# A two-layer encoder trunk: residual stream kept feature-major, with the RMS factor of each token taken as a column sum on TensorE

## The chip, the cores and the metric

One core of a Trainium2 chip. The metric is the device time of one execution of the whole program in microseconds. The engines have their own instruction queues and run side by side: TensorE (PE, with its weight loads listed apart as PEld), VectorE (DVE), ScalarE (ACT), GpSimd (POOL), and SyncE (SP), which here only issues DMAs. Each queue is worked through in order; waits between queues are semaphores.

## The reference

512 tokens of 1024 features, two layers, float32. Every layer is

```
xn = rmsnorm(x, norm_g[i])
y = mixer(xn)                 # layer 0: neighbourhood attention, layer 1: latent attention (MLA)
h = x + y
gate = sigmoid(rmsnorm(h, ple_norm[i]) @ ple_w_gate[i])
x = h + gate * (p[i] @ ple_w_proj[i])
```

and the output is `rmsnorm(x, final_norm)`, where rmsnorm divides each token by the root of its mean square over the 1024 features and multiplies by a gain per feature. Either mixer projects xn to its operands and to z (1024 wide), runs 16 heads, multiplies the 1024 outputs by silu(z) and projects back: `(o * silu(z)) @ w_out`. Layer 0 takes q, k, v from one projection and attends within a window of 8 x 16 on a grid of 8 x 64 tokens. MLA takes a rank-384 and a rank-256 code and a rotary key from xn, norms the codes, and projects them to 16 heads of q (64 + 32 rotary), k and v.

## The kernel before, in words

Every float32 product is made of three matmuls in the rounded format F32R: each operand is split into hi (an ACT copy that rounds) and lo (the rest, a subtraction), and hi·hi, hi·lo and lo·hi are added in PSUM. `load_w` (L67) loads a weight tile of 512 KB on SP's queue, copies hi on ACT (whi, L76) and subtracts lo on POOL (wlo, L77); the buffers are three deep. A product of 128 output rows, 512 columns and 1024 in the sum is 24 matmuls (`proj_T`, L133).

PSUM has eight banks: two for projections ("mm"), two for scores ("S"), three for transposes ("T") and one for head outputs ("O").

Two layouts are in use. Activations that are to be multiplied stand feature-major, [128 features, 512 tokens] times 8 (`xT`, `oT`, each as hi and lo). The residual stream, `res`, stands token-major, four tiles [128 tokens, 1024 features], since a token's square sum is then one ACT instruction with an accumulator (`inv_rms`, L100: ACT square, DVE scale, POOL power), and its factor a scalar per partition. So `rows_to_cols` (L125) and `turn_h` (L612) turn token tiles by TensorE transposes, four to a PSUM bank, with a hi copy on ACT and a lo subtraction on DVE for each bank: 32 transposes for xn of layer 0, 64 for h of both layers (`hg`), 32 for x between the layers (`x1n`).

The program runs thus. **Start** (L579): the operands of PLE(0), x and the gain row g0 are loaded; xn is made and turned; PLE (p @ w_proj) is written to DRAM through `pe`; five z tiles of layer 0 follow (`z_phase`, L144). **Neighbourhood attention** (`na_heads`, L182): per pair of heads, project v, q and k, then two heads; the last three z tiles come behind the last projections. Each pair ends in `combine` (ACT and DVE, L157) and `gated` (L166: POOL multiply by z, ACT hi, POOL lo), which makes one of eight `oT` tiles. **out_proj**: token tiles t by halves n of the output; in the first half four tiles are open, over both "mm" and both "S" banks, and the terms run by weight chunk (`by_chunk`), with order bound by `issue_after` to the last projection. Each result is added to `res` (L361) and turned. **gate_phase**: 8 products per layer, the sigmoid on ACT with the token's factor as its scale (L401), times pe (L402), added to `res` (L404). In layer 0 `done` (L630) then norms and turns x; in layer 1 (L640) it sums squares half by half, scales and writes the output, the last tile in two pieces of 256. **MLA**: `mla_c` makes the codes, norms and turns them (cn) and moves the rotary key rows into two sets of operand buffers by DMAs on SP (`move`, L89); `mla_heads` (L535 on) makes seven z tiles, then group(0) and project(0) (rope on ACT, DVE, POOL; moves of the rotated rows into qe and qo), the eighth z tile, and the heads with the next projections between them.

The tile framework puts instructions into each engine's queue by its own simulated timeline, within the data dependences; `reuse_waits` lets buffers be taken over across pools with waits on the tiles alone.

## Time and profile before

| | us |
|---|---|
| median of three runs | 691.66 (690.6 to 692.21) |
| profiled execution | 690.26 |
| its span | 688.5, granted TensorE clock 0.998 |

The span is from the first to the last recorded event; the other 1.8 us lie outside the recorded events. The profile divides it thus, by windows of the trace (idle is the window less PE's busy time):

| window, us | what runs | PE busy | PE idle |
|---|---|---|---|
| 0 to 21 | loads, PLE(0), xn and its transposes | 11.76 | 9.24 |
| 21 to 54 | rest of PLE(0), five z tiles | 32.97 | 0.03 |
| 54 to 253 | neighbourhood attention | 198.92 | 0.08 |
| 253 to 358 | out_proj and gates of layer 0, codes begin | 104.67 | 0.33 |
| 358 to 433 | codes, z tiles, first projections of MLA | 72.45 | 2.55 |
| 433 to 585 | MLA heads | 147.97 | 4.03 |
| 585 to 677 | out_proj and gates of layer 1 | 91.67 | 0.33 |
| 677 to 689 | last tile, final norm, output | 4.03 | 7.97 |

In a row of the groups, the line, engine and operation are followed by output and inputs with shapes and the count; then the busy time, the mean length of one in ns, and the engine's idle time just before, with what ended it. A row of the chain is a start, a length and what ran. A row of a timeline is the same with the idle time before it in brackets. In the windows each engine has its busy time and count; after the five engines stand the granted clock, the DMA engines' share, and GB/s.

### The profile page before, as it was taken

The numbers are of one execution on the slowest core, as the hardware profiler recorded it, in microseconds if no ns is written. First come the engines' busy times: TensorE is split into PE (matmuls) and PEld (weight loads), VectorE is DVE, ScalarE is ACT, GpSimd is POOL, SyncE is SP. The second block draws the span as 40 slices with busy tenths as digits, with TensorE's granted clock in tenths as the row PEclk, the third lists the DMA queues.
The fourth block names the chain that finished last, engine by engine and source line by source line (L and its number), as shares of the span: only waits on it lengthen the run. The fifth ranks groups of instructions, "written<-read, shape, count | busy, mean of one in ns | idle before, by whom it ended". The sixth has DMA issues, their size and how long they took to land.

```text
span 688.5 us, 10118 instructions
## 1 busy us (share of the span) xinstructions
PE 664.4 (97%) x3580; PEld 566.9 (82%) x3580; DVE 356.3 (52%) x813; ACT 402.1 (58%) x799; POOL 396.7 (58%) x309
## 2 busy tenths in 40 slices
PE   5999999999999999999999998999999999999995
PEld 4789898998988888788899886787888777887885
DVE  4300364647737624633524503788988886055333
ACT  6722576666767562643443634878888878426433
POOL 1753557467575565853044634777789867658511
PEclk9999999999999999999999999999999999999999
DMA  8731423323223127544243344203121201584122
GB/s 324 234 121 62 133 86 104 105 72 97 85 92 108 40 97 301 167 130 135 89 104 107 107 121 116 81 23 93 24 70 37 86 1 68 191 308 154 61 77 92
DMA packets 28642, 77.53 MB, mean 113 GB/s; under 512 B 3632, under 2 KB 6704, under 8 KB 28592
## 3 DMA queue, kind: packets, MB, share of 16 engines
q1 hardware_dynamic: 28592, 76.89, 33.9%
q8 instruction: 28, 0.46, 0.3%
q14 instruction: 22, 0.18, 0.1%
HBM read 65.34 MB, written 8.39 MB: 107 GB/s over the span
## 4 chain that ended last, share of the span: by engine, by line
PE 86%; ACT 5%; DVE 4%; issue 2%; DMA 1%; POOL 1%; SPq 0%; POOLq 0%; DVEq 0%; ACTq 0%
PE ps_mm L96 63%; PE ps_S L96 9%; PE ps_T L122 5%; PE ps_O L96 4%; PE ps_O L335 2%; PE ps_T L323 1%; ACT ex L561 1%; ACT whi L76 1%; DMA x<-x 1%; PE ps_S L288 1%; PE ps_S L287 1%; DVE mx L559 1%; POOL wlo L77 0%; DVE mx L301 0%; ACT pt_hi L83 0%
## 5 line engine op out<-in xcount | busy, mean ns | idle before, releaser
L77 POOL TENSOR_TENSOR wlo<-wraw,whi 128x1024 fp32r<-128x1024 f32 (+3 forms) x96 | 218.3, 2287 | 118.5 <-ACT whi L76 68.4
L76 ACT ACTIVATE whi<-wraw 128x1024 fp32r<-128x1024 f32 (+4 forms) x100 | 97.9, 988 | 97.0 <-PE ps_mm L96 32.1
L563 POOL TENSOR_TENSOR ex<-ex,rc 128x512 f32<-128x512 f32 x64 | 66.2, 1048 | 20.7 <-DVE rc L562 13.9
L96 PE MATMUL ps_mm<-whi,hnT 128*128 128x512 f32 (+1 forms) x272 | 69.7, 377 | 0.0
L96 PEld LDWEIGHTS ps_mm<-whi,hnT 128*128 128x128 f32 x272 | 49.5, 188 | 9.5
L310 POOL TENSOR_TENSOR ex<-ex,rc 128x128 f32<-128x128 f32 (+1 forms) x64 | 34.3, 560 | 38.1 <-DVE rc L306 36.5
L559 DVE TENSOR_REDUCE mx<-ps_S 128x1 f32<-128x512 f32 x64 | 43.7, 685 | 15.3 <-PE ps_S L96 14.3
L96 PE MATMUL ps_mm<-xh,whi 128*128 128x512 f32 x192 | 50.9, 398 | 0.1
L96 PE MATMUL ps_mm<-xh,wlo 128*128 128x512 f32 x192 | 49.1, 391 | 0.0
L561 ACT ACTIVATE ex<-ps_S,mx 128x512 f32<-128x512 f32 x64 | 44.1, 689 | 8.2 <-DVE mx L559 6.7
L96 PE MATMUL ps_mm<-xl,whi 128*128 128x512 f32 x192 | 48.6, 392 | 0.0
L85 DVE TENSOR_TENSOR pt_lo<-ps_T,pt_hi 128x512 fp32r<-128x512 f32 x64 | 43.0, 679 | 5.0 <-ACT pt_hi L83 4.6
L305 ACT ACTIVATE ex<-ex,mx 128x128 f32<-128x128 f32 (+1 forms) x64 | 30.2, 473 | 22.0 <-DVE mx L301 21.6
L106 POOL TENSOR_TENSOR rs<-ss,half 128x1 f32<-128x1 f32 x24 | 13.0, 549 | 50.3 <-DVE ss L105 49.0
L96 PEld LDWEIGHTS ps_mm<-xl,whi 128*128 128x128 f32 x192 | 35.6, 188 | 7.3
L96 PEld LDWEIGHTS ps_mm<-xh,wlo 128*128 128x128 f32 x192 | 35.6, 188 | 7.0
L83 ACT ACTIVATE pt_hi<-ps_T 128x512 fp32r<-128x512 f32 x64 | 37.0, 597 | 7.6 <-PE ps_T L122 7.3
L96 PE MATMUL ps_mm<-wlo,hnT 128*128 128x512 f32 (+1 forms) x136 | 40.6, 379 | 0.0
L96 PEld LDWEIGHTS ps_mm<-xh,whi 128*128 128x128 f32 x192 | 34.5, 188 | 6.4 <-ACT z L152 0.4
L122 PE MATMUL ps_T<-ident,ex 128*128 128x128 f32 x256 | 36.3, 273 | 0.2 <-DVE pt_lo L85 0.2
L122 PEld LDWEIGHTS ps_T<-ident,ex 128*128 128x128 f32 x256 | 30.7, 141 | 6.8 <-issue 0.7
L85 DVE TENSOR_TENSOR vt<-ps_mm,vt 128x256 fp32r<-128x256 f32 x32 | 13.2, 415 | 44.3 <-ACT vt L83 44.0
(215 smaller groups left out, 1579.7 us busy)
## 6 DMA issues: line engine op xcount, KB each, us to landing
pe<-pe SPq DMA_DIRECT2D x32, 256.0 KB, 2.9
wraw<-na_qk SPq DMA_DIRECT2D x16, 512.0 KB, 3.4
wraw<-gate SPq DMA_DIRECT2D x16, 512.0 KB, 3.4
wraw<-na_z SPq DMA_DIRECT2D x8, 512.0 KB, 4.2
wraw<-na_v SPq DMA_DIRECT2D x8, 512.0 KB, 3.3
wraw<-na_o SPq DMA_DIRECT2D x8, 512.0 KB, 3.4
wraw<-mla_z SPq DMA_DIRECT2D x8, 512.0 KB, 4.2
wraw<-mla_o SPq DMA_DIRECT2D x8, 512.0 KB, 3.6
```

The costliest lines, as they stand in the source:

```text
L76: nc.scalar.activation(hi[:, c], raw[:, c], AF.Copy)
L77: (rest or nc.gpsimd).tensor_tensor(out=lo[:, c], in0=raw[:, c], in1=hi[:, c].bitcast(F32), op=ALU.subtract)
L83: nc.scalar.activation(hi, src, AF.Copy, scale=scale)
L85: nc.vector.tensor_tensor(out=lo, in0=src, in1=hi.bitcast(F32), op=ALU.subtract)
L96: last = nc.tensor.matmul(out, l, r, start=i == 0, stop=i == n - 1)
L122: self.nc.tensor.transpose(t[:, i * P:(i + 1) * P], b, self.ident)
L305: self.last_exp = nc.scalar.activation(e, e, AF.Exp, bias=mx[:, qt:qt + 1], accum_out=sm[:, qt:qt + 1])
L310: nc.gpsimd.tensor_tensor(out=e, in0=e, in1=rc[:, qt:qt + 1].to_broadcast([P, e.shape[1]]), op=ALU.mult)
L335: nc.tensor.matmul(O[:, o:o + w], vh[kt], s[:, c:c + w], start=n == 0, stop=n == 7, skip_group_check=True)
L559: nc.vector.reduce_max(mx[:, c], sp, axis=AX.X, negate=True)
L561: nc.scalar.activation(ex, sp, AF.Exp, bias=mx[:, c], accum_out=sm[:, c])
L563: nc.gpsimd.tensor_tensor(out=ex, in0=ex, in1=rc[:, c].to_broadcast([P, S]), op=ALU.mult)
```

## The change

The residual stream is kept feature-major throughout: `res` is [128 features, 8, 512 tokens], x comes in turned from the host and the output goes out turned (the host turns it back). No token tile is turned on TensorE any more. The square sum of a token is now a sum over partitions: squares of the eight feature tiles are added elementwise into `acc` [128, 512] (`add_square`: ACT square, POOL add, DVE add for the last), and `col_rms` multiplies hi and lo of `acc`, as the stationary operand, by a column of ones, two matmuls for each 128 tokens with two moving columns; then come DVE (add epsilon), POOL (power -0.5), and one transpose per 128 tokens of the factor spread over 128 columns, which gives the factor with tokens along the columns, the same on every partition. This `R` is multiplied in on DVE; the missing root of 1024 is the scale 32. Gains are now scalars per partition (`gains`), where they were rows broadcast over partitions by DMA.

So the products for z and the gates run on unnormalised operands (gain times x, or times h), and R is multiplied into the result on DVE before the silu or sigmoid. At the start the first two z tiles are interleaved by pairs of feature tiles and run on raw x; xn is made from x, gain and R only for q, k and v. out_proj, PLE and gate weights are laid out by output column tile of 128 features, so the weights are the stationary operand: `out_proj` opens the first two column tiles together (both "S" banks), interleaved by pairs of `oT` tiles (`by_k`), then goes one tile at a time. PLE uses "mm" and "S" banks in turn. The gate phase of layer 1 runs the last three column tiles in two blocks of 256 tokens, and the output of a block is multiplied by its factor straight from PSUM, two feature tiles to an instruction, and written. In MLA the first two z tiles come ahead of `mla_c`; the rotary key rows are moved into set 0 from the slabs and from set 0 into set 1, after project(0). `ple_load(0)` returns three operands, of which the start drops the third and loads it again behind the fourth tile of x.

```diff
+    def add_square(self, pool, acc, src, first, fast=False):
+        nc = self.nc
+        if first:
+            nc.scalar.activation(acc, src, AF.Square)
+            return
+        sq = pool.tile([P, S], F32, name="sq", tag="sq", bufs=2)
+        sq = sq[:, :src.shape[1]]
+        nc.scalar.activation(sq, src, AF.Square)
+        (nc.vector if fast else nc.gpsimd).tensor_tensor(out=acc, in0=acc, in1=sq, op=ALU.add)
+    def col_rms(self, pool, acc, R=None):
+        nc = self.nc
+        n = acc.shape[1]
+        nt = n // P
+        ah = pool.tile([P, S], F32R, name="ah", tag="ah", bufs=1)[:, :n]
+        al = pool.tile([P, S], F32R, name="al", tag="al", bufs=1)[:, :n]
+        nc.scalar.activation(ah, acc, AF.Copy)
+        nc.vector.tensor_tensor(out=al, in0=acc, in1=ah.bitcast(F32), op=ALU.subtract)
+        ps = self.psum("T")
+        for t in range(nt):
+            self.mms(ps[:, 2 * t:2 * t + 2], [(a[:, t * P:(t + 1) * P], self.ones) for a in (ah, al)])
+        rc = self.small.tile([P, NT], F32, name="rcol", tag="rcol", bufs=4)[:, :nt]
+        nc.vector.tensor_scalar(rc, win(ps, 0, P, 0, [[2, nt]]), D * EPS, None, op0=ALU.add)
+        nc.gpsimd.tensor_tensor(out=rc, in0=rc, in1=self.half.to_broadcast([P, nt]), op=ALU.pow)
+        turned = self.transposes([rc[:, t:t + 1].to_broadcast([P, P]) for t in range(nt)])[:, :n]
+        if R is None:
+            return rc, turned
+        nc.scalar.activation(R, turned, AF.Copy)
+        return rc, R
...
+    def proj_T2(self, outs, ws, parts):
+        n = [0] * len(outs)
+        for i, part in enumerate(parts):
+            for o, (out, w) in enumerate(zip(outs, ws)):
+                for l, r in part(w):
+                    self.nc.tensor.matmul(out, l, r, start=n[o] == 0, stop=n[o] == 23)
+                    n[o] += 1
+    def by_k(self, xT):
+        return [lambda w, k=k: self.terms(w, xT, range(k, k + 2)) for k in range(0, KD, 2)]
...
+        def finish(j, ps):
+            z = zs[j] = R if R is not None and j == 7 else self.zp.tile([P, S], F32, name="z", tag="z")
+            with self.tc.issue_after(after) if after is not None else nullcontext():
+                if R is None:
+                    nc.scalar.activation(z, ps, AF.Silu)
+                else:
+                    nc.vector.tensor_tensor(out=z, in0=ps, in1=R, op=ALU.mult)
+                    nc.scalar.activation(z, z, AF.Silu, scale=32.0)
...
     def out_proj(self, wap, oT, res, after, last_mm):
         nc = self.nc
...
+        def finish(j, ps):
+            nc.vector.tensor_tensor(out=res[:, j, :], in0=ps, in1=res[:, j, :], op=ALU.add)
+            after(j)
+        ws = [self.load_w(wap[j], 1024) for j in range(2)]
+        pss = [self.psum("S") for j in range(2)]
+        with self.tc.issue_after(last_mm):
+            self.proj_T2(pss, ws, self.by_k(oT))
+        for j in range(2):
+            finish(j, pss[j])
+        for j in range(2, KD):
+            w = self.load_w(wap[j], 1024, extra=True)
+            ps = self.psum("mm")
+            self.proj_T(ps, w, oT)
+            finish(j, ps)
...
     def ple_load(self, layer):
         early = dict(parts=2, rest=self.nc.vector) if layer == 0 else {}
-        return (self.load_w(self.a["pT"][layer], 1024, **early),
-                self.load_w(self.a["proj"][layer, 0], 1024, **early))
+        return [self.load_w(ap, 1024, **early)
+                for ap in (self.a["pT"][layer], self.a["proj"][layer, 0], self.a["proj"][layer, 1])]
...
+    def gate_phase(self, pool, layer, hT, Rh, res, after, blocks):
         nc, a = self.nc, self.a
...
+        def load(j):
+            w = self.load_w(a["gate"][layer, j], 1024, extra=True)
+            pe = pool.tile([P, S], F32, name="pe", tag="pe", bufs=3)
+            nc.sync.dma_start(pe, self.pe[layer][j])
+            return w, pe
+        def tile_(j, w, pe, c):
+            n = c.stop - c.start
+            ps = self.psum("mm")[:, :n]
+            xT = [[g[:, :, c] for g in s] for s in hT]
+            if j == 0:
+                self.mms(ps, [t for k in range(0, KD, 2) for t in self.terms(w, xT, range(k, k + 2))])
+            else:
+                self.proj_T(ps, w, xT)
+            sg = pool.tile([P, S], F32, name="sg", tag="sg", bufs=2)[:, :n]
+            nc.vector.tensor_tensor(out=sg, in0=ps, in1=Rh[:, c], op=ALU.mult)
+            nc.scalar.activation(sg, sg, AF.Sigmoid, scale=32.0)
+            nc.vector.tensor_tensor(out=sg, in0=pe[:, c], in1=sg, op=ALU.mult)
+            r = res[:, j, c]
+            nc.vector.tensor_tensor(out=r, in0=r, in1=sg, op=ALU.add)
+            after(j, c)
+        nl = 0
+        for j in range(KD):
+            if len(blocks(j)) == 1:
+                tile_(j, *load(j), blocks(j)[0])
+                nl = j + 1
+        if nl < KD:
+            ws = {j: load(j) for j in range(nl, KD)}
+            for b in range(2):
+                for j in range(nl, KD):
+                    tile_(j, *ws[j], blocks(j)[b])
...
+        for s, sl in enumerate((slab_h, slab_l)):
+            self.move(sets[0]["ke"][s][64:96], sl[64:96])
+            self.move(sets[0]["ko"][s][0:64], sl[0:64])
+            self.move(sets[0]["qo"][s][0:32], sl[0:32])
...
-        zs = self.z_phase(a["mla_z"], xT, range(NEARLY))
+        zs.update(self.z_phase(a["mla_z"], xT, range(2, NEARLY), R=self.r1))
         group(0)
         last = project(0)
-        zs.update(self.z_phase(a["mla_z"], xT, range(NEARLY, 8)))
+        for s in range(2):
+            for n, r in (("ke", slice(64, 96)), ("ko", slice(0, 64)), ("qo", slice(0, 32))):
+                self.move(sets[1][n][s][r], sets[0][n][s][r])
+        zs.update(self.z_phase(a["mla_z"], xT, range(NEARLY, 8), R=self.r1))
...
+            operands = self.ple_load(0)[:2]
+            nc.sync.dma_start(self.gains[:, :40], a["gains"])
+            nc.vector.tensor_scalar(self.gains[:, 40:], self.gains[:, :40], 32.0, None, op0=ALU.mult)
             nc.sync.dma_start(self.ident, a["ident"])
...
+            raw, xT = pair("r"), None
+            part = lambda T, k: [T[s][k // 4][:, k % 4, :] for s in range(2)]
+            acc = pool.tile([P, S], F32, name="acc", bufs=1)
+            xs = []
+            for k in range(KD):
+                if k == 4:
+                    operands.append(self.load_w(a["proj"][0, 1], 1024, parts=2, rest=nc.vector))
+                x = pool.tile([P, S], F32, name="x", tag="x", bufs=8)
+                nc.sync.dma_start(x, a["xT"][k])
+                xs.append(x)
+                hi, lo = part(raw, k)
+                nc.scalar.activation(hi, x, AF.Copy, scale=self.gain(0, k))
+                nc.vector.scalar_tensor_tensor(lo, x, self.gain(0, k), hi.bitcast(F32), op0=ALU.mult, op1=ALU.subtract)
+                sq = acc if k == 0 else pool.tile([P, S], F32, name="sq", tag="sq", bufs=2)
+                nc.gpsimd.tensor_tensor(out=sq, in0=x, in1=x, op=ALU.mult)
+                if k:
+                    nc.vector.tensor_tensor(out=acc, in0=acc, in1=sq, op=ALU.add)
             self.ple(pool, 0, "pe", 3, operands)
-        zs = self.z_phase(a["na_z"], xT, range(8 - NLATE))
-        oT = ([self.bigtile(f"oh{g}") for g in range(2)], [self.bigtile(f"ol{g}") for g in range(2)])
+            R = pool.tile([P, S], F32, name="R", bufs=1)
+            self.col_rms(pool, acc, R)
+            zs = self.z_phase(a["na_z"], raw, range(2), parts=self.by_k(raw), R=R)
+            xT = pair("x")
+            for k in range(KD):
+                hi, lo = part(xT, k)
+                nc.vector.scalar_tensor_tensor(xs[k], xs[k], self.gain(0, k, True), R, op0=ALU.mult, op1=ALU.mult)
+                nc.scalar.activation(hi, xs[k], AF.Copy)
+                nc.gpsimd.tensor_tensor(out=lo, in0=xs[k], in1=hi.bitcast(F32), op=ALU.subtract)
+            zs.update(self.z_phase(a["na_z"], raw, range(2, 8 - NLATE), R=R))
...
+                def done_h(j):
+                    turned(hT, j, 2 + layer)
+                    self.add_square(pool, acc, res[:, j, :], j == 0, j == KD - 1)
+                self.out_proj(a["na_o"] if layer == 0 else a["mla_o"], oT, res, done_h, last)
+                self.col_rms(pool, acc, Rh)
+                acc2 = pool.tile([P, S], F32, name="acc2", bufs=1)
                 if layer == 0:
+                    x1T = pair("x1")
+                    def done(j, c):
+                        turned(x1T, j, 1)
+                        nc.sync.dma_start(self.spill[j], res[:, j, :])
+                        self.add_square(pool, acc2, res[:, j, :], j == 0)
+                    blocks = lambda j: [slice(0, S)]
+                else:
+                    def done(j, c):
+                        r = res[:, j, c]
+                        self.add_square(pool, acc2[:, c], r, j == 0, j == KD - 1)
+                        nc.scalar.activation(r, r, AF.Copy, scale=self.gain(4, j, True))
+                        if j < KD - 1:
                             return
+                        R2 = self.col_rms(pool, acc2[:, c])[1]
+                        R2 = bass.AP(tensor=R2.tensor, offset=R2.offset, ap=[list(R2.ap[0]), [0, 2], list(R2.ap[1])])
+                        for i in range(0, KD, 2):
+                            o = res[:, i:i + 2, c]
+                            nc.vector.tensor_tensor(out=o, in0=o, in1=R2, op=ALU.mult)
+                            nc.sync.dma_start(a["out"][i:i + 2, :, c].rearrange("j p t -> p j t"), o)
+                    blocks = lambda j: [slice(0, S)] if j < 5 else [slice(0, 256), slice(256, S)]
+                self.gate_phase(pool, layer, hT, Rh, res, done, blocks)
+                if layer == 0:
+                    self.r1 = self.zp.tile([P, S], F32, name="r1", tag="z")
+                    self.r1c = self.col_rms(pool, acc2, self.r1)[0]
```

224 lines of the change are left out of this document (71 added, 153 removed).

## The prediction

> **What bounds the kernel now.** I read the page's busy shares and chain first, then the windows, the chain in order of time for the price of a matmul in a stream, the groups by shape for the other engines, and the timeline at the places where the change puts a wait.
>
> ```profile
> span 688.5 us, 10118 instructions
> PE 664.4 (97%) x3580; PEld 566.9 (82%) x3580; DVE 356.3 (52%) x813; ACT 402.1 (58%) x799; POOL 396.7 (58%) x309
> PE 86%; ACT 5%; DVE 4%; issue 2%; DMA 1%; POOL 1%; SPq 0%; POOLq 0%; DVEq 0%; ACTq 0%
> ```
>
> TensorE is busy for 97% of the span and holds 86% of the chain; no other engine passes 58%. So the time is the PE stream plus its holes, and an edit counts by what it takes from the stream or by a hole it opens or closes. The windows (PE, PEld, DVE, ACT, POOL; clock; DMA) say where the holes are:
>
> ```profile
> 0.00:10.00 10.00, 3.25 (x8) 2.64 (x9) 2.93 (x6) 4.95 (x7) 0.63 (x5) 1.00 0.78 259
> 10.00:21.00 11.00, 8.51 (x48) 6.09 (x46) 8.52 (x12) 9.83 (x19) 4.92 (x6) 1.00 0.79 319
> 253.00:261.00 8.00, 8.00 (x41) 6.77 (x40) 0.69 (x1) 4.07 (x5) 5.61 (x4) 1.00 0.76 285
> 261.00:299.00 38.00, 37.67 (x180) 31.03 (x179) 22.08 (x27) 17.94 (x25) 28.61 (x15) 1.00 0.58 206
> 299.00:358.00 59.00, 59.00 (x301) 51.81 (x300) 23.67 (x35) 21.57 (x33) 15.98 (x14) 1.00 0.34 106
> 585.00:637.00 52.00, 51.67 (x242) 42.61 (x241) 19.83 (x25) 23.90 (x32) 34.42 (x18) 1.00 0.62 218
> 677.00:689.00 12.00, 4.03 (x34) 3.83 (x32) 4.21 (x11) 4.05 (x10) 1.82 (x3) 0.86 0.23 87
> ```
>
> From the end of neighbourhood attention (253) through both gate phases PE hardly waits: 0, 0.33, 0 and 0.33 us in four of these windows. The holes are the start (9.2 us in the first 21) and the tail (8 us of 12). A version that stalls PE a microsecond where it is now full loses that microsecond whole.
>
> The price of a removed or added matmul is what the chain pays for it, not its own length, since matmuls overlap:
>
> ```profile
> 82.82 5.47 PE ps_mm L96 x24
> 177.16 2.88 PE ps_mm L96 x24
> 274.52 0.88 PE ps_T L122 x8
> 253.16 0.92 PE ps_O L335 x8
> L122 PE MATMUL ps_T<-ident,hg 128*128 128x128 f32 x64 | 9.0, 272 | 0.0
> L122 PE MATMUL ps_T<-ident,x1n 128*128 128x128 f32 x32 | 4.1, 272 | 0.0
> ```
>
> 512 columns cost 5.47/24 = 0.228 us, 256 columns 2.88/24 = 0.120, a transpose 0.88/8 = 0.110, though one transpose lasts 272 ns.
>
> **The change, part by part.** *Removed transposes.* Of 128, the 32 of xn belong to the start (below); the 64 of hg and 32 of x1n stood in a full PE stream: 96 x 0.110 = **-10.6**. The Trainium skill ("TensorE: Matmul & The Clock Gate", Part 4: PE-mode transpose) gives about 275 ns for a transpose in a kernel; this trace agrees for a single one (272). Charged that way the removal would be 96 x 0.272 = 26 us; the row of eight in 0.88 speaks against it, and I go by that.
>
> *Added column RMS on PE.* Three times in the stream (h of each layer, x1): 4 transposes of the factor (0.44) and 8 matmuls with 2 moving columns, which the trace does not show. Below, they are nearly free; above, each costs as much as a 128-column transpose: 0.88. I take 0.75, near the upper end, as each needs its weights loaded: 3 x 1.2 = **+3.6** (1.3 to 4.0).
>
> *Start.* Now the PE leaves PLE(0), 32 transposes and five z tiles at:
>
> ```profile
> 6.75 0.80 PE L96 MATMUL ps_mm<-whi 128*128 128x512 f32 x1 [6.75 <-ACT whi L76]
> 7.77 0.63 PE L96 MATMUL ps_mm<-whi 128*128 128x512 f32 x1
> 8.20 0.63 PE L96 MATMUL ps_mm<-whi,wlo 128*128 128x512 f32 x1
> 17.85 5.50 POOL L77 TENSOR_TENSOR wlo<-wraw,whi 128x1024 fp32r<-128x1024 f32 x2 [0.42 <-ACT whi L76]
> 53.85 1.12 PE L96 MATMUL ps_mm<-whi,xh 128*128 128x256 f32 x8
> ```
>
> After, z0 and z1 run on raw x behind PLE with no transpose between. From 6.75: 48 PLE matmuls 10.9, an estimated 4 for the slow opening (8.20 - 7.77 = 0.43 a matmul) and for waits on x and weights, z0 and z1 10.9 (to 32.5). z2 needs one of the two "mm" banks, which come free only after R (an ACT copy) and a DVE multiply, and the whi copy of z4 is ahead of R on ACT: a hole of 2. Then z2 to z4, 16.4: v may start at 51. Gain **-2.8**. POOL is what can spoil it: behind the end of z1 (32.5) and the whi copy of z4 it has that tile's wlo, eight xl (1.3 each, as ol below) and the two wlo of v, the three at 2.4 to 2.75 from the row at 17.85: done near 33.6 + 10.4 + 7.7 = 51.7, and v's first tile asks for the last of them about 2 us after its start at 51, 53. Ends: nothing gained, if v waits 3 us, and -5, if the 2 us hole closes. The second projection half is loaded twice (512 KB more, its first copies unused); the g0 broadcast of the same size is gone.
>
> *End of neighbourhood attention.* After the last ps_O (253.00 to 254.08) comes the chain that makes the last oT pair:
>
> ```profile
> 254.12 0.59 ACT L162 ACTIVATE u<-ps_O 64x512 f32<-64x512 f32 x1 [2.13 <-PE ps_O L335]
> 254.74 0.69 DVE L163 TENSOR_TENSOR u<-ps_O,u 64x512 f32<-64x512 f32 x1 [4.58 <-ACT u L162]
> 255.51 1.28 POOL L168 TENSOR_TENSOR u<-u,z 128x512 f32<-128x512 f32 x1 [1.65 <-DVE u L163]
> 256.83 0.63 ACT L171 ACTIVATE oh<-u 128x512 fp32r<-128x512 f32 x1 [2.12 <-POOL u L168]
> 257.54 1.30 POOL L172 TENSOR_TENSOR ol<-u,oh 128x512 fp32r<-128x512 f32 x1 [0.74 <-ACT oh L171]
> ```
>
> hi is ready 3.4 us (257.46) after that ps_O, lo 4.8. Before, four token tiles share six out_proj weight chunks, and the terms of earlier heads cover it (window 253 to 261: no idle). After, only two column tiles are open, and in PE's order just 4 matmuls (0.9 us) that do not need the last pair stand behind ps_O; about three more fit between hi and lo. Hole: 4.8 - 0.9 - 0.8 = **+3.1** (1.5 to 4). At the end of MLA 37 matmuls (8.4 us) stand there: nothing.
>
> *h of each layer.* The chain from the last h tile to its factor runs under gate tiles 0 and 1 (48 matmuls, 10.9 us) but its four transposes stand behind both in PE's order, and tile 2 needs a bank that only Rh frees. On ACT a whi copy that waits for the end of tile 1 is ahead of the Rh copy:
>
> ```profile
> L76 ACT ACTIVATE whi<-wraw 128x1024 fp32r<-128x1024 f32 x80 | 83.8, 1058 | 78.4 <-PE ps_mm L96 20.5 <-issue 17.6 <-DMA wraw<-mla_o 15.7
> L83 ACT ACTIVATE hnT<-ps_T 128x512 fp32r<-128x512 f32 x16 | 9.3, 592 | 8.6 <-PE ps_T L122 8.6
> L361 DVE TENSOR_TENSOR r<-ps_mm,r 128x512 f32<-128x512 f32 x12 | 7.9, 686 | 38.8 <-PE ps_mm L96 38.8
> L106 POOL TENSOR_TENSOR rs<-ss,half 128x1 f32<-128x1 f32 x24 | 13.0, 549 | 50.3 <-DVE ss L105 49.0 <-PE ps_mm L96 1.3
> ```
>
> Hole: 1.06 + 0.59 + 0.69 and handovers 0.1, less the transposes counted above (0.44) = 2.0, twice **+4.0** (1.0 to 2.6 each; the low end if the whi copy finds its buffer free). For x1 the transposes stand within a projection tile and two z tiles cover the chain: **+0.2**.
>
> *MLA start.* The first scores with the low part of q now stand before z7 instead of behind it and wait for the rope move. Before, PE idled 0.68 there, and the low part was used 7 us later:
>
> ```profile
> pe<-pe SPq DMA_DIRECT2D x32, 256.0 KB, 2.9
> 421.89 1.28 POOL L491 TENSOR_TENSOR rl<-xr,rh 128x512 fp32r<-128x512 f32 x1 [0.74 <-ACT rh L490]
> 424.10 1.45 PE L96 MATMUL ps_S<-ke,qe 96*128 96x512 f32 x4 [0.68 <-ACT ke L83]
> 424.30 0.59 SPq L90 DMA_DIRECT2D qo<-rl  x1
> ```
>
> The set-0 moves on SP go first, those of set 1 behind them; the low half is written at 423.2, and a move issued then lands within 2.9 us, the time for four times its bytes; I take 2 to 2.5, so 425.5 on this clock, while the scores that need it could start a microsecond before. With only 7 matmuls (1.6 us) between the last cn transposes and the q projection, against 55 before, I take **+1.1** (0 to 2.5). Two more activation-table loads fall in this stretch; other ACT work has slack there.
>
> *Smaller.* Three gate tiles of layer 1 run as 256-column halves, 144 x 0.120 = 17.3, where before two whole tiles and a split one took 48 x 0.228 + 48 x 0.120 = 16.7: **+0.6**. The 0.3 us waits of each out_proj are gone: **-0.7**. The gain broadcasts (2 x 1 MB) hid under DMA shares of at most 0.76.
>
> *Tail.* Now, after the last matmul (near 681.0):
>
> ```profile
> 681.07 0.47 ACT L401 ACTIVATE sg<-ps_mm,rs 128x256 f32<-128x256 f32 x1 [0.19 <-PE ps_mm L96]
> 682.03 0.42 DVE L404 TENSOR_TENSOR r<-r,sg 128x256 f32<-128x256 f32 x1
> 682.55 0.42 ACT L646 ACTIVATE sq<-r 128x256 f32<-128x256 f32 x1 [1.01 <-DVE r L404]
> 683.39 0.55 POOL L653 TENSOR_TENSOR rs<-mn,half 128x1 f32<-128x1 f32 x1 [1.71 <-DVE mn L647]
> 683.97 0.72 ACT L657 ACTIVATE r<-r,rs 128x512 f32<-128x512 f32 x1 [0.91 <-POOL rs L653]
> 685.14 0.38 SPq L658 DMA_DIRECT2D out<-r  x1
> ```
>
> 7.5 us to the span's end, 3.4 of it from the last issue. After: a DVE multiply by Rh (0.4, sigmoid beside what follows), then on DVE's queue the four output multiplies of block 0 (512 elements, 0.69 each: 2.8) ahead of the last tile's pe multiply, which stands still for them; multiply and add 0.85; square 0.45; add 0.45; ah and al 0.9; 4 small matmuls 0.5; rcol 0.25; power 0.6; 2 transposes 0.4; four multiplies 2.8; the last DMA 3.4 plus handovers 0.2: 14.0. **+6.5** (4.6 if the block 0 multiplies slip into a gap, 7.5 if shared memory ports slow DVE).
>
> *Sum:* -10.6 + 3.6 - 2.8 + 3.1 + 4.0 + 0.2 + 1.1 + 0.6 - 0.7 + 6.5 = +5.0 on the profiled execution of 690.26 (span 688.5): 695.3. The median of the runs shown, 691.66, lies 1.4 above that execution; half of this goes on top: **696**.
>
> **The rivals.** (1) *A removed transpose is worth more than its share of a run* (faster). Its place is every point where four of them broke the stream, with a weight load each. It decides from 0.110 + 5.0/96 = 0.162 us a transpose: above that the change is no loss. At the full 272 ns the sum falls by 96 x 0.162 = 15.6: **680**. For: the length of one. Against: eight in 0.88, and 0.33 us of idle in a window with half of them.
>
> (2) *POOL late at the start* (slower still). If its 1.3 and 2.4 stretch by a tenth to a fifth beside a busier DVE, as the two wlo in 5.50 have done, xl and v's wlo end 3 to 4 us later, v waits for them, and start's -2.8 becomes +1; a tail with the same slowing costs 1 more: **701**.
>
> (3) *The clock drops behind a hole* (slower still). The opening, after idling, runs a matmul in 0.43 instead of 0.228, and the last window shows 0.86 with an idle PE. Were PE to run 3 us at half rate behind the three long holes (attention's end, two gates), each would cost 1.5 more: **700**. The Trainium skill ("TensorE: Matmul & The Clock Gate", Why this matters for your kernels) wants no idle gap over about 3 us between bursts; the trace of before has no such gap in mid-stream, so it cannot tell.
>
> (4) *The low ends together* (faster): column matmuls nearly free (1.5), attention's hole 1.5, gates 1.0 each, MLA start 0, tail 4.6: -10.6 + 1.5 - 2.8 + 1.5 + 2.0 + 0.6 - 0.7 + 4.6 = -3.9: **687**. For: DVE and ACT have slack in the windows. Against: each hole follows from an order of queues and two banks, not from load.
>
> (5) *No net effect*: holes at the gates at their low end and block 0's multiplies out of the way, the rest as forecast: 5.0 - 2.0 - 1.9 = +1.1: **692**.
>
> **How the numbers follow.** Forecast 0.52; (1) 0.06; (2) 0.09; (3) 0.08; (4) 0.13; (5) 0.12. A change under 0.2% (1.4 us) cannot be told from none. Faster: (1), (4) and a little of the forecast's low side, 0.20; same: (5), 0.13; slower: the rest, 0.67. The forecast's own range is 693 to 700; down to (4) and up through (2) and (3) it is 687 to 701.5.
>
> **What would show it.** Right: transposes of h, x1n and xn gone from the groups; PE idle of about 2 us before gate tile 2 in both layers, ended by DVE's multiply by Rh; about 3 us behind the last ps_O ended by POOL's ol; 14 us behind the last matmul with four DVE multiplies ahead of the last pe multiply; the first v matmul near 51. Wrong: no idle at the gates; a tail under 11 us; v near 54 or later, waiting for POOL; a clock under 0.95 in any window but the first and last.

## The result and the profile after

The changed kernel takes 715.5 us (median of four runs, 713.03 to 715.76) against 691.75 for the kernel before in the same session: a ratio of 1.0338 (1.0312 to 1.0364). It is slower, as forecast, but by 24 us where 5 were forecast, far above the range. The profiled execution took 713.03, span 711.3; it is the fastest of the four (the others 715.26 to 715.76). The page after:

```profile
span 711.3 us, 10190 instructions
PE 667.3 (94%) x3560; PEld 567.3 (80%) x3560; DVE 404.1 (57%) x841; ACT 420.9 (59%) x816; POOL 444.4 (62%) x332
```

PE's busy time hardly moved (664.4 before), though 96 transposes left its stream. DVE gained 48 us and POOL 48. The windows, cut as before:

```profile
10.00:21.00 11.00, 9.98 (x38) 7.83 (x37) 10.68 (x12) 9.37 (x16) 7.31 (x6) 1.00 0.99 328
21.00:54.00 33.00, 26.96 (x115) 21.24 (x113) 25.79 (x20) 15.02 (x22) 27.66 (x15) 0.95 0.40 134
...
358.00:433.00 75.00, 69.12 (x389) 62.06 (x387) 29.52 (x84) 32.92 (x66) 37.84 (x27) 0.98 0.34 102
689.00:712.00 23.00, 9.81 (x74) 8.99 (x72) 11.03 (x25) 5.80 (x13) 3.05 (x4) 0.72 0.27 92
```

Before, PE was full from 21 to 54, with DVE almost at rest; the row of before is

```profile
21.00:54.00 33.00, 32.97 (x148) 27.31 (x149) 1.98 (x3) 14.37 (x19) 18.72 (x11) 1.00 0.56 185
```

Now 6 us are idle there, at a lower clock (0.95). From 358 to 433 idle rose from 2.55 to 5.88 (the same window now holds work that lies up to 8 us earlier in the kernel). The span divides thus between landmarks of PE's timeline:

| stretch | before | after | difference |
|---|---|---|---|
| start to first v matmul | 53.85 | 59.63 | +5.8 |
| neighbourhood attention | 199.95 | 200.06 | +0.1 |
| last ps_O to first gate matmul, layer 0 | 40.27 | 40.17 | -0.1 |
| first gate matmul to first codes or z matmul on x1 | 45.84 | 48.35 | +2.5 |
| from there to the first MLA scores | 84.2 | 90.1 | +5.9 |
| MLA heads | 164.4 | 164.6 | +0.2 |
| out_proj, layer 1 | 48.05 | 45.28 | -2.8 |
| gates, layer 1 | 44.5 | 48.43 | +3.9 |
| behind the last product | 7.5 | 14.7 | +7.2 |

The timeline of the start shows why v is late:

```profile
19.60 0.68 DVE L682 TENSOR_TENSOR acc<-acc,sq 128x512 f32<-128x512 f32 x1
21.81 2.82 POOL L79 TENSOR_TENSOR wlo<-wraw,whi 128x1024 fp32r<-128x1024 f32 x1
22.31 2.86 DVE L682 TENSOR_TENSOR acc<-acc,sq 128x512 f32<-128x512 f32 x1
28.36 2.83 POOL L79 TENSOR_TENSOR wlo<-wraw,whi 128x1024 fp32r<-128x1024 f32 x1
29.06 2.68 DVE L682 TENSOR_TENSOR acc<-acc,sq 128x512 f32<-128x512 f32 x1
31.77 0.63 ACT L135 ACTIVATE ah<-acc 128x512 fp32r<-128x512 f32 x1 [6.63 <-DVE acc L682]
32.45 0.27 PE L98 MATMUL ps_T<-ones,ah 128*128 128x2 f32 x1 [2.04 <-ACT ah L135]
33.79 1.06 PE L182 MATMUL ps_mm<-rl,whi 128*128 128x512 f32 x2
54.07 2.08 PE L98 MATMUL ps_mm<-rh,whi 128*128 128x512 f32 x8 [1.14 <-ACT xh L691]
```

One add of two tiles in SBUF takes 0.68 us while POOL stands idle, and 2.86 or 2.68 when it meets a running POOL subtraction: it ends at 25.17 and 31.74, 0.54 and 0.55 behind the ends of POOL's instructions (24.63, 31.19). So it seems not to run slowly but to stand until POOL's instruction is over, and then to take little less than its usual time. The Trainium skill ("SBUF — State Buffer", Who interferes with whom) says that a DVE instruction with two SBUF inputs contends with a GpSimd instruction that reads SBUF, through a port pair that is locked exclusively, and that one with at most one SBUF input (outside the two-port modes) does not. These rows agree with the first half (ends 0.54 and 0.55 behind POOL's); the second is tried below. Behind the wait of 2.04 two matmuls take 0.85 (33.79 to the next at 34.64): half rate, until about 37. The last wait of the stretch (54.07) is put down to the hi part of xn, but the product that waits does not read xn. It needs a bank, which DVE's multiply of z2 (L199, begun at 53.24) frees, and that stands on DVE behind the eight multiplies by R (42.20 to 53.3). These met POOL in the same way: the groups give 1458 ns for L690, where the row of L678 at 25.10, of the same shape and begun beside an idle POOL, is 0.74 us.

At the start of MLA:

```profile
426.50 0.42 SPq L539 DMA_DIRECT2D rope_c<-rope_c  x1
430.90 0.69 DVE L565 TENSOR_TENSOR xr<-xr,rope_c 128x512 f32<-128x512 f32 x1 [4.89 <-DMA rope_c<-rope_c]
431.51 0.75 DVE L87 TENSOR_TENSOR vt<-ps_mm,vt 128x256 fp32r<-128x256 f32 x2
431.98 2.93 PE L98 MATMUL ps_mm<-cT,whi 128*128 128x512 f32 x6 [4.94 <-DVE vt L87]
```

The rope table is asked for at 426.50; on SP's queue it stands behind the six slab moves and two weight loads, and the moves wait for the last code transposes (418.67). Before, these stood at 399.81, the table was asked for at 411.07, and there was work enough for PE until it came:

```profile
411.07 1.50 SPq L459 DMA_DIRECT2D rope_c<-rope_c  x1
```

In the changed kernel DVE's rope multiply waits 4.89 us for it, the split of v is behind that multiply on DVE, and PE waits 4.94 for the split, then runs at half rate again.

The holes that were forecast, and the tail:

```profile
263.38 0.50 PE L182 MATMUL ps_S<-oh,whi 128*128 128x512 f32 x1 [2.50 <-ACT oh L231]
313.94 2.13 PE L98 MATMUL ps_mm<-hh,whi 128*128 128x512 f32 x8 [1.41 <-DVE sg L468]
325.81 2.12 PE L98 MATMUL ps_mm<-hh,whi 128*128 128x512 f32 x8 [0.44 <-DVE sg L468]
662.20 2.12 PE L98 MATMUL ps_mm<-hh,whi 128*128 128x512 f32 x8 [1.41 <-DVE sg L468]
697.11 2.47 DVE L742 TENSOR_TENSOR res<-res,ps_T 128x512 f32<-128x512 f32 x4
699.50 0.42 DVE L470 TENSOR_TENSOR sg<-pe,sg 128x256 f32<-128x256 f32 x1
701.98 0.37 PE L98 MATMUL ps_T<-ones,ah 128*128 128x2 f32 x1 [5.03 <-ACT ah L135]
705.00 2.48 DVE L742 TENSOR_TENSOR res<-res,ps_T 128x512 f32<-128x512 f32 x4 [1.56 <-PE ps_T L158]
```

They are where the prediction put them (the first is ended by ACT's oh, and POOL's ol ends only another 0.17), as is the order on DVE's queue in the tail: four multiplies of block 0, and then the last pe multiply.

### The profile page after: what moved, and what is told of

It is laid out like the page before. It is cut to its first block, busy times and chain, and to the rows that moved or that the text cites. A ratio compares the mean times of both kernels' runs of the same rounds, so it can differ in the third digit from the quotient of the medians.

```text
span 711.3 us, 10190 instructions
## 1 busy us (share of the span) xinstructions
PE 667.3 (94%) x3560; PEld 567.3 (80%) x3560; DVE 404.1 (57%) x841; ACT 420.9 (59%) x816; POOL 444.4 (62%) x332
## 5 line engine op out<-in xcount | busy, mean ns | idle before, releaser
L125 POOL TENSOR_TENSOR acc<-acc,sq 128x512 f32<-128x512 f32 (+1 forms) x27 | 36.0, 1332 | 41.5 <-ACT sq L124 41.5
L98 PE MATMUL ps_mm<-xh,whi 128*128 128x512 f32 x152 | 41.3, 401 | 0.0
L98 PE MATMUL ps_mm<-xh,wlo 128*128 128x512 f32 x152 | 39.2, 392 | 0.0
L98 PE MATMUL ps_mm<-xl,whi 128*128 128x512 f32 x152 | 38.7, 392 | 0.0
L98 PE MATMUL ps_mm<-hh,whi 128*128 128x512 f32 (+1 forms) x152 | 34.6, 362 | 3.3 <-DVE sg L468 3.3
L158 PE MATMUL ps_T<-ident,ex 128*128 128x128 f32 x256 | 36.6, 272 | 0.0
L98 PE MATMUL ps_mm<-cT,whi 128*128 128x512 f32 x104 | 30.2, 417 | 5.6 <-DVE vt L87 4.9
L98 PE MATMUL ps_mm<-hl,whi 128*128 128x512 f32 (+1 forms) x152 | 35.0, 361 | 0.0
L98 PE MATMUL ps_mm<-hh,wlo 128*128 128x512 f32 (+1 forms) x152 | 34.0, 359 | 0.0
L714 DVE SCALAR_TENSOR_TENSOR hl<-res,gains,hh 128x512 fp32r<-128x512 f32 x16 | 26.8, 1678 | 10.9 <-ACT hh L713 10.7
L98 PEld LDWEIGHTS ps_mm<-hh,whi 128*128 128x128 f32 x152 | 25.7, 188 | 8.6 <-DVE sg L468 4.2
```

The lines of the kernel that those rows point to most:

```text
L98: last = nc.tensor.matmul(out, l, r, start=i == 0, stop=i == n - 1)
L125: (nc.vector if fast else nc.gpsimd).tensor_tensor(out=acc, in0=acc, in1=sq, op=ALU.add)
L158: self.nc.tensor.transpose(t[:, i * P:(i + 1) * P], b, self.ident)
```

## The experiments

Times are medians beside runs of the kernel before on the same chip (691.2 to 691.6); ratios have 95% intervals. Unless said otherwise an edit is made to the changed kernel alone.

**The start without POOL's squares.** The squares go to ACT, and the wlo of z0 and z1 to DVE.

```diff
-                nc.gpsimd.tensor_tensor(out=sq, in0=x, in1=x, op=ALU.mult)
+                nc.scalar.activation(sq, x, AF.Square)
...
+            zs = self.z_phase(a["na_z"], raw, range(2), parts=self.by_k(raw), R=R, rest=nc.vector)
```

> The changed kernel with one thing moved at the start: the eight squares of x on ACT instead of POOL, and the low parts of the z0 and z1 weights on DVE instead of POOL, so that POOL has almost nothing to read from SBUF until R is made. Theory (a DVE instruction with two SBUF inputs stands still until the POOL instruction that is running has ended): the adds into acc take 0.7 us instead of 2.7 to 2.9, ah is ready some 6 us earlier than 32.4, z2 starts near 35 instead of 41.7, the first v matmul near 52 instead of 59.6, and the whole takes 706 to 709 instead of 713 to 715.5. Rival A (x lands late, the DMA engines being 0.99 busy from 10 to 21): R comes no earlier, first v stays within 1 us of 59.6. Rival B (ACT is the slow engine there): ACT has 5 us more to do and first v comes later than 59.6.

712.65 us, 1.0307 (1.0288 to 1.0326). The groups of this run:

```profile
L682 DVE TENSOR_TENSOR acc<-acc,sq 128x512 f32<-128x512 f32 x7 | 4.8, 686 | 0.3 <-ACT sq L680 0.2
L690 DVE SCALAR_TENSOR_TENSOR x<-x,gains,R 128x512 f32<-128x512 f32 x8 | 12.1, 1580 | 0.0
```

The adds are at 686 ns (1524 in the changed kernel), but v starts at 56.34, where near 52 was expected, and the time misses its range: the multiplies by R (two SBUF inputs, beside POOL's xl) still take 1580, and PE waits 1.47 (37.49) and 2.14 us (50.80) for banks that DVE's multiplies of z free, the second again behind the multiplies by R. A new wait of 2.03 on ACT's copies of pe stands in PLE (22.14), as ACT has more to do. So the adds are one cause, and the multiplies are left.

**The old start in the changed kernel.** Token-major norm and 32 transposes as before, the rest unchanged. It was meant to undo the start.

```diff
-            R = pool.tile([P, S], F32, name="R", bufs=1)
-            self.col_rms(pool, acc, R)
-            zs = self.z_phase(a["na_z"], raw, range(2), parts=self.by_k(raw), R=R)
...
+                self.rms(xn, xt[t], g0, D)
...
+        zs = self.z_phase(a["na_z"], xT, range(8 - NLATE))
```

> The changed kernel with the start of before: x loaded by tokens beside the turned one, xn normed and turned by 32 transposes, PLE, then five z tiles on the normed operand. Everything behind the first v matmul stays as changed. Theory (the start costs 5.8 us and nothing of it is owed to later stages): first v near 54, 707 to 710. What is then left over before, 16 to 18 us, belongs to the other parts. Rival (the late start only shifts waits that would come anyway in neighbourhood attention): 713 to 715.

711.05 us, 1.0284 (1.0263 to 1.0305), above the 707 to 710 expected; v starts at 57.33, not near 54. The undo did not give the old start, since the tile framework set other work beside it:

```profile
19.47 2.35 POOL L79 TENSOR_TENSOR wlo<-wraw,whi 128x1024 fp32r<-128x1024 f32 x1
19.54 3.36 DVE L109 SCALAR_TENSOR_TENSOR xn<-x,rs,g 128x1024 f32<-128x1024 f32 x1
23.55 0.66 PE L158 MATMUL ps_T<-ident,xn 128*128 128x128 f32 x4 [3.36 <-DVE xl L87]
```

The scaling of xn, two tiles in SBUF, stands behind a POOL subtraction here too (1.28 alone), and PE waits 3.36. So as a price of the new start this run is inconclusive; it shows the same wait in another instruction.

**The start with the multiply reading PSUM.** On top of the first experiment xn's multiply takes R from its PSUM bank, z2 and z3 use the score banks, and PLE's third operand is loaded once.

```diff
-  ...scalar_tensor_tensor(xs[k], xs[k], self.gain(0, k, True), R, ...)
+  ...scalar_tensor_tensor(xs[k], xs[k], self.gain(0, k, True), self.turned, ...)
...
-            ps = self.psum("mm")
+            ps = self.psum("S" if banks and j % 4 >= 2 else "mm")
```

> As the first experiment (squares on ACT, low parts of the z0 and z1 weights on DVE), and three things more at the start: xn is made with R read from PSUM, so that this DVE instruction has one SBUF input only; z2 and z3 take score banks; the third PLE operand is loaded once. Theory: in the first experiment the lock-step of DVE and POOL at xn remained (eight multiplies at 1.7 us each, where one alone takes 0.74), and so did the wait for a bank. Now the multiplies take about 0.75 each, no hole before z2, first v at 51 to 53 (56.3 in the first experiment, 59.6 changed), 706.5 to 709.5. Rival (ACT, with its copies, squares and hi parts, has become the limit): first v at 55 or later.

705.76 us, 1.0207 (1.0189 to 1.0224). Its group, its window and the first v:

```profile
L691 DVE SCALAR_TENSOR_TENSOR x<-x,gains,ps_T 128x512 f32<-128x512 f32 x8 | 5.3, 741 | 0.0
```

```profile
21.00:54.00 33.00, 33.00 (x166) 27.92 (x164) 13.23 (x18) 18.32 (x27) 22.53 (x14) 1.00 0.46 145
```

```profile
50.30 1.11 PE L98 MATMUL ps_mm<-whi,xh 128*128 128x256 f32 x8
```

The same operation, with one operand moved from SBUF to PSUM, falls from 1580 to 741 ns. PE is full, and v starts at 50.30, a little earlier than expected. Three edits act together here (PSUM operand, banks, one load less); only the length of the multiply is tied to one of them. Neighbourhood attention gives 1.0 of the gain back (201.0 us, from 200.06).

**Rope tables early.** Their two loads move to the beginning of the MLA part.

```diff
-        nc.sync.dma_start(rc_t, a["rope_c"])
-        nc.sync.dma_start(rs_t, a["rope_s"])
...
+                for r, n in zip(self.rope, ("rope_c", "rope_s")):
+                    nc.sync.dma_start(r, a[n])
                 zs = self.z_phase(a["mla_z"], x1T, range(2), parts=self.by_k(x1T), R=self.r1)
```

> The changed kernel with the two loads of the rope tables issued at the beginning of the MLA part instead of behind the six slab moves and two weight loads on SP. Theory (the tables land at 430.9, DVE's queue stands at the rope multiply, the v split behind it is late, PE waits 4.94 us for its bank and then runs at half rate for some 4 us): both go, first scores near 432 instead of 438.3, 706 to 709 in all. Rival A (the slab itself, made late by the last transposes of the codes, is what everything waits for): a hole of 3 us or more stays. Rival B (the move of the rotated rows takes its place): a new wait of 2 us or more before the first scores.

709.83 us, 1.0261 (1.0243 to 1.0278), just above what was expected. The first scores are at 434.98 where near 432 was expected, but this execution came to MLA 2.0 us later. The stretch from the first matmul on x1 to the scores falls from 90.1 to 84.7, a wait of 1.36 is left of the 4.94, and no half rate follows:

```profile
429.64 0.75 PE L98 MATMUL ps_mm<-whi,cT 128*128 128x256 f32 x4 [1.36 <-DVE vt L87]
430.46 1.55 PE L98 MATMUL ps_mm<-cT,whi 128*128 128x512 f32 x6
```

Six matmuls are recorded with 1.55, with 2.93 behind the wait of 4.94. The late tables were the cause.

**Four banks for the gates.**

```diff
-            ps = self.psum("mm")[:, :n]
+            ps = self.psum("mm" if j % 4 < 2 else "S")[:, :n]
```

> The changed kernel with four PSUM banks for the gate tiles in turn (two of the score banks beside the two of the projections), nothing else. Theory (tile 2 waits for a bank that the multiply by Rh frees): the holes of 1.41 and 0.44 us in layer 0 and 1.41 in layer 1 go, 3.3 us in all, 710 to 712. Rival (the factor itself is late): the holes move to tile 4 and nothing is gained.

712.41 us, 1.0289 (1.0251 to 1.0327), just above what was expected. The waits of 1.41 and 0.44 are gone; the stage of layer 0 falls from 48.35 to 46.06, that of layer 1 by 1.6. The MLA part is ordered otherwise by the tile framework: the stretch up to the first scores falls by 2.0, although it ends in a wait of 3.29 on a move of q's rows, and the heads give 3.9 back (164.6 to 168.5), with a granted clock of 0.57 for some 4 us behind that wait (435 to 439) and half rate again behind one of 1.96.

**Four open column tiles in out_proj**, two more in the "mm" banks.

```diff
-        pss = [self.psum("S") for j in range(2)]
+        pss = [self.psum("S" if j < 2 else "mm") for j in range(4)]
```

> The changed kernel with four column tiles of out_proj open together instead of two (both score banks and both projection banks). Theory (only 4 matmuls that do not need the last pair of heads stand behind the last ps_O): the hole of 2.50 us in layer 0 goes, 712 to 713.5 where the changed kernel takes 713 to 715.8. Rival (the weights of the third and fourth tile come late): a hole of 2 us or more stays, waiting for whi or wlo.

711.11 us, 1.0286 (1.0262 to 1.031), a little better than expected. The wait of 2.50 is gone, and the stretch from the last ps_O to the first gate matmul is 36.6, from 40.2.

**Block 0's output behind the last factor.** The four multiplies go behind the epsilon instruction of block 1.

```diff
+        if late is not None:
+            with self.tc.issue_after(last.ins):
+                late()
...
-                        R2 = self.col_rms(pool, acc2[:, c])[1]
+                        R2 = self.col_rms(pool, acc2[:, c], late=held.pop() if held else None)[1]
```

> The changed kernel with the four output multiplies of the first block put behind the scaling of the second block's factor on DVE, so that they run while the factor is raised and turned; nothing else. Theory (2.47 us of multiplies stand ahead of the last tile's chain, of which the gap for power and transposes hides about 1.4): the stretch from the end of the last product to the end of the span falls from 14.7 us to about 13.3, 711.5 to 714. Rival (the chain is the same length whatever the order, since the multiplies only change place on DVE): no difference, 14.7.

714.12 us, 1.0327 (1.0308 to 1.0346). A near miss: the tail is 14.3, and 13.3 was expected.

```profile
700.35 0.37 PE L98 MATMUL ps_T<-ones,ah 128*128 128x2 f32 x1 [3.21 <-ACT ah L135]
702.47 5.01 SPq L748 DMA_DIRECT2D out<-res  x8
```

The column matmuls wait 3.21 instead of 5.03, but now all eight output DMAs are issued in one row, 0.63 each, and SP ends last.

**All five together** (the start of the third, rope, gates, out_proj, tail):

> All at once: the start of the experiment before this one, the rope tables loaded early, four banks for the gates, four open tiles in out_proj, the first block's output multiplies put back. If the causes are the ones named and add up: 715.5 - 7 - 5.7 - 3.3 - 2.5 - 1.4 = 695.6, between 693 and 699; what is then left over before is mostly the longer tail. Rival (the parts share the same time, or the planner's new order of the MLA part opens other holes): 700 or more.

690.93 us, 0.9995 (0.9986 to 1.0004): no difference from before, and below the 693 to 699 expected. The five gains taken alone, by the medians, 9.7 + 5.7 + 3.1 + 4.4 + 1.4 = 24.3, would give 691.2, so they add up within the spread of the medians. By the spans of the profiled executions they would not (14.2 of 22.0).

**A shorter tail on top.** The last tile's squares go to PE as a third term of the column matmuls, rounded to F32R without a low part, and so skip the add and the split; two multiplies of block 0 stand behind the last add, two behind the epsilon.

```diff
+                            nc.scalar.activation(sq, r, AF.Square)
+                            more = (sq,)
...
-  ... for a in (ah, al)])
+  ... for a in (ah, al, *more)])
```

> The version with all causes mended, with another tail: the squares of the last tile's second block go straight to the column matmuls as a third term (rounded, without a low part), so that the add into acc and the split of acc leave the chain behind the last product, and two of the first block's four output multiplies go into the gap behind the last add, the other two behind the scaling of the factor. The time of the version with all causes mended was 690.9, with 13.9 us from the end of the last product to the end of the span. Theory (these three steps, about 1.4 us, and the two multiplies that delayed the second block's, about 0.7, are on the path): 11.5 to 12.3 us behind the last product, 688.3 to 689.7 in all, faster than before (691.2). Rival (the eight output DMAs, 0.6 us each on SP, set the end): 690.3 or more.

687.67 us, 0.9947 (0.9933 to 0.996), better than expected. The tail is 11.0.

**The price of a matmul.** The table above leaves 4 us in out_proj and gates open: holes of 2.7 + 1.85 + 1.41, 80 transposes less (-8.8; 16 more lie in the next stretch), two column RMS (+2.4), halves (+0.6) and the old waits (-0.7) make -0.5, while the four stretches sum to +3.5. The rows of the changed kernel, a z tile of MLA and a gate tile:

```profile
319.62 2.02 PE L98 MATMUL ps_mm<-hh,whi 128*128 128x512 f32 x8
321.48 2.02 PE L98 MATMUL ps_mm<-hl,whi 128*128 128x512 f32 x8
...
393.52 1.98 PE L98 MATMUL ps_mm<-x1l,whi 128*128 128x512 f32 x8
395.33 0.84 PE L98 MATMUL ps_mm<-x1h,whi 128*128 128x512 f32 x3
```

Eight matmuls take 1.86 in a gate (319.62 to 321.48) and 1.81 in a z tile. The operations have the same shape; the operands lie elsewhere. As the program places them, gate weights and most of out_proj's come from a second set of buffers, which starts 128 bytes off a multiple of 256, while hh, oh and the first set start on a multiple. In the kernel before all had the same remainder, 160. First 128 bytes of padding ahead of the second set:

```diff
         self.small = ec(tc.tile_pool(name="small", bufs=8))
+        self.pad = self.small.tile([P, 32], F32, name="pad", tag="pad", bufs=1)
```

> In the changed kernel eight 512-column matmuls of out_proj and the gates take 1.86 us in a run, where the same form in its z tiles (and everywhere in the kernel before) takes 1.81 to 1.82. The tiles that the program places from the out_proj pool on (the extra weight buffers, the codes cT) start 128 bytes off a multiple of 256, while the operands they meet (hh, oh, and the other weight buffers) start on a multiple of 256; before, all started at the same remainder, 160. This kernel only adds 128 bytes of padding ahead of those pools, so that all start on a multiple of 256. Theory: the two operands of a matmul at different remainders of 256 cost 0.006 us a matmul. Then eight take 1.82 in out_proj and gates, 28 products of 24 matmuls gain 28 x 24 x 0.0055 = 3.7 us, the projections from cT some tenths more: 710 to 712.5 against 715.5, both gate stages about 1.1 shorter. Rival: the rate comes from what runs beside these phases (weights' loads and splits, five deep) and not from addresses: eight still take 1.86 and the time stays within 1 us of 715.5.

709.55 us, 1.0261 (1.0241 to 1.0282), just below what was expected.

```profile
319.47 1.98 PE L100 MATMUL ps_mm<-hh,whi 128*128 128x512 f32 x8
321.28 1.98 PE L100 MATMUL ps_mm<-hl,whi 128*128 128x512 f32 x8
```

Eight take 1.81. In layer 1 out_proj falls from 45.28 to 44.42 and the gates from 48.43 to 48.01, 1.3 together. Eleven products of 512 columns at 24 x 0.0058 less would be 1.5; the three gate tiles in halves gain nothing, since eight 256-column matmuls take 0.94 to 0.96 in both kernels. In the gates of layer 0 another wait opens (1.32), and that stretch gains nothing; the queues hold the same instructions in the same order as in the changed kernel, save for the padding, so it is no matter of order. Then the same padding ahead of everything, so that the first set and the activations are off by 128 and the second set is not:

```diff
         self.gains = self.const.tile([P, 80], F32, name="gains")
+        self.pad = self.const.tile([P, 32], F32, name="pad")
```

> The same 128 bytes of padding one place earlier: now the feature-major operands and the common weight buffers start 128 off a multiple of 256, and the extra weight buffers and cT on a multiple. If it is the difference between the two operands that costs, nothing changes: 1.86 for eight in out_proj and gates, 1.82 in z tiles, time 714 to 717. If a start 128 off a multiple of 256 is slow by itself, z tiles and the projections of both attentions slow to 1.86 as well, and some 1500 more matmuls cost 0.0055 each: 721 to 725.

713.5 us, 1.0318 (1.0289 to 1.0347), just below what was expected.

```profile
320.15 2.03 PE L100 MATMUL ps_mm<-hh,whi 128*128 128x512 f32 x8
322.02 2.02 PE L100 MATMUL ps_mm<-hl,whi 128*128 128x512 f32 x8
...
403.71 2.07 PE L100 MATMUL ps_mm<-x1h,whi 128*128 128x512 f32 x8
405.62 1.98 PE L100 MATMUL ps_mm<-x1l,whi 128*128 128x512 f32 x8
407.44 0.84 PE L100 MATMUL ps_mm<-x1h,wlo 128*128 128x512 f32 x3
```

Gates are at 1.87, z tiles (405.62 to 407.44, both operands off by 128) at 1.82. So it is not the remainder itself that costs but that the two operands differ in it. The two padded kernels differ in nothing but the place of the padding, and their medians by 3.95 us.

**The fastest version with the padding:**

> The fastest kernel so far (687.67: all five repairs and the shorter tail) with the padding of 128 bytes ahead of the out_proj pool. Theory of the operands' remainders: 3.5 to 4.5 less, 683 to 684.5, with 1.82 for eight in out_proj and gates. Rival (not addresses): 687 to 688.5.

684.87 us, 0.9899 (0.9882 to 0.9915): 1% faster than before, and below the version without padding (0.9933 to 0.996). The gain of 2.8 is under the 3.5 to 4.5 expected: the heads of MLA lose 1.4, with a granted clock of 0.57 from 504 to 508.

## Why the prediction was right in sign and wrong in size

**Removed transposes, column RMS: right.** Transposes were worth about their share of the stream. Out_proj of layer 1 shows it best: at the old price of a matmul (the padding ahead of the second set) it takes 44.42, from 48.05 before, of which 0.33 was a wait. It records 28 transposes before and none after, and as good as the same other matmuls, which makes about 0.12 a transpose: near the 0.110 taken, under the 0.162 of rival 1. Two-column matmuls follow each other every 0.11 us in the timeline (309.09, 309.20, 309.31), which is the 0.88 that was the upper end for eight.

**End of neighbourhood attention and gates: right.** 3.1 was forecast and 2.50 + 0.17 measured; 2.0 a gate, and 1.41 + 0.44 and 1.41 measured. Removing each removed its wait. What the first of them costs behind it is another matter (rival 3 below).

**Tail: right.** 14.0 forecast, 14.7 measured, with the four multiplies ahead of the last one, as told.

**Start: the term that failed most**, -2.8 forecast and +5.8 measured. The step gave z2 a hole of 2 for R, its copy and one multiply, took the adds into acc and the eight multiplies by R as done in time, and looked for the danger in POOL (rival 2, stretched "by a tenth to a fifth"). The runs show DVE standing for the rest of a running POOL instruction: an add of 0.68 takes 2.86. The first v is late, the prediction's own sign of being wrong, but through DVE rather than through POOL's xl and wlo. The profile of before had the sign of it, in a pair of groups of one shape that the prediction did not read:

```profile
L615 DVE TENSOR_TENSOR hg<-r,gp 128x512 f32<-128x512 f32 x16 | 24.2, 1530 | 2.8 <-PE ps_T L122 2.8
L404 DVE TENSOR_TENSOR r<-r,sg 128x512 f32<-128x512 f32 x15 | 10.4, 692 | 0.5
```

The same operation at 1530 beside one at 692 asks what runs beside it. The trace of before answers: one hg at 274.09, with POOL idle, takes 0.69, and one at 288.18 takes 2.17 and ends 0.54 behind POOL's subtraction (287.40, 2.41 long). Without most of these meetings v starts at 50.30, near the 51 of the sum. That agreement is partly luck: the start of that run also has no wait for a bank, and without its hole of 2 the sum would give about 49.

**MLA start: the second.** +1.1 forecast, +5.9 measured. (The stretch of 5.9 also loses 16 transposes and gains one column RMS, so what failed there is rather larger.) The step named the cover that went, 7 matmuls in place of 55 behind the last code transposes, but followed only the rope move, which comes last. The rope tables, behind the slab moves on SP in both kernels, lost the same cover and are needed earlier.

**The price of a matmul, the third.** The prediction took 0.228 for matmuls whose operands the change places anew. Of the 28 products with weights of the second set three run in halves and do not pay; the other 25, of 24 matmuls each at 0.0058 more, are 3.5 us.

**Rival 3 was right about one of its three holes, and the profiled execution hides it.** PE ran at half rate behind waits of 2.04 and 4.94, which it had not named, and behind the gates' 1.41 in no run. Behind the wait of 2.50 after neighbourhood attention PE kept its rate in the profiled execution of the changed kernel (first row), but not in that of the run with early rope tables, which has the same wait (second row):

```profile
263.00:267.00 4.00, 3.45 (x14) 2.51 (x15) 1.23 (x2) 3.69 (x5) 3.60 (x2) 1.00 0.99 329
264.00:268.00 4.00, 3.65 (x9) 2.63 (x10) 0.60 (x1) 3.13 (x4) 3.63 (x3) 0.62 1.02 358
```

Of the nine profiled executions that have this wait (2.48 to 2.50), two kept a granted clock of 1.00 behind it and seven had 0.57 to 0.62 in a window of 4 us behind it. The stretch up to the gates takes 40.0 and 40.2 in the two, 41.2 to 41.6 in six of the seven, and 40.8 in the one whose matmuls are cheaper (the first with padding). So the hole usually costs 1.0 to 1.6 more than its length, and rival 3 had put 1.5 on it. What decides between the two is not shown. It may be part of the 2.5 between the profiled execution of the changed kernel and its median; the other three executions, with lower granted clocks (0.977 to 0.982 against 0.984), have no trace.

Together the three failed terms are 8.6 + 4.8 + 3.5 = 16.9 of the 17.8 us between forecast and span (+5.0 and +22.8).

## What to carry to other kernels

Before an elementwise step is moved to DVE beside a busy POOL, look in the groups for one shape with two mean times; if its operands are both in SBUF, keep one of them in PSUM or give the work to ACT. List every DMA that a moved block issues and what stands ahead of it on the queue. When buffers move, compare the cadence of matmuls of one shape across stages: a few per cent there outweighs a hole. Before a hole is priced from one trace, look at the same hole in other runs: here it cost its own length in two of them and 1.0 to 1.6 us more in the others.

## What the runs showed of the hardware that was not expected

A 512-column matmul costs 0.2325 us in a run instead of 0.2267 when its two operands start 128 bytes apart modulo 256 (1.86 and 1.81 for eight, switched on and off by 128 bytes of padding); a 256-column one does not (0.94 to 0.96 for eight either way). Other distances were not tried. A DVE instruction with two SBUF inputs took 1580 ns on average beside POOL, and 741 with one of them in PSUM. Behind one and the same wait of 2.50 us PE ran at half rate for some 3 us in seven profiled executions (granted clock 0.57 to 0.62 in the 4 us behind it) and at full rate in two.
